# Transposing the feed-forward activations with VectorE blocks and DRAM transfers instead of TensorE

## The chip, the core and the metric

The kernel runs on one core of a Trainium2 chip. Its engines work side by side, each through its own queue of instructions in order: TensorE (PE; PEld is its weight load), VectorE (DVE), ScalarE (ACT), GpSimd (POOL) and SyncE (SP). Transfers are issued from SP's and GpSimd's queues and carried out by the core's 16 DMA engines. An instruction that needs another engine's result, or a transfer's, waits for a semaphore at the head of its queue, and all that stands behind it waits too. The metric is the device time of one execution in microseconds (us).

## The reference

One layer of a diffusion transformer: 256 latent tokens and 256 context tokens of width 2048. Modulated norms, one input projection, two kinds of attention, an output projection, and at the end a gated feed-forward block, which the change concerns:

```python
def swiglu_sublayer(x, shift, scale, gate, norm_g, w_ff_gate, w_ff_up, w_ff_down):
    h = modulate(rms_norm(x, norm_g), shift, scale)
    return x + gate * ((jax.nn.silu(h @ w_ff_gate) * (h @ w_ff_up)) @ w_ff_down)
```

Here h is 256 x 2048, w_ff_gate and w_ff_up are 2048 x 5632, w_ff_down is 5632 x 2048, all float32.

## The kernel before

**Matrix products.** Each product is made of three fast ones: a float32 operand is split into a rounded part "hi" and the rest "lo", and hi x hi, hi x lo and lo x hi are added up in PSUM (lines L236, L237 and L238 in `mm3`). A weight tile of 256 rows x 512 columns is loaded by SP into one of seven buffers `wraw`; ScalarE casts it to `whi` (L231) and VectorE subtracts to `wlo` (L232), three buffers each. The activations are kept transposed, split in hi and lo by `split` (ScalarE L241, VectorE L242).

**One projection.** `project` goes through a product of 256 tokens x 512 columns. A *step* is one weight tile: 2 blocks of 128 rows x 2 token halves (tk 0 and 1) x 3 matmuls = 12 matmuls. With 2048 rows that are 8 steps. At the end `evac` takes the two PSUM tiles. After each step `tick` counts down the work that `after(n, fn)` has put off by n steps, and runs what is due.

**The feed-forward stage.** It goes through 11 groups of 512 columns (cg). In each, `project(w_g)` and `project(w_u)` are 8 steps each: `g_evac` writes silu of the gate product to `act[tk]` (ScalarE), `u_evac` multiplies the up product into it (VectorE). `act[tk]` is 128 tokens x 512 columns, and the down product needs it the other way round, with the columns on the partitions. `turn`, two or three steps later, does that: four TensorE transposes of 128x128 into one PSUM tile `ftp` (L990), then `split` from there into the group's tile `fT`, 512 columns x 128 tokens for each tk. The down product w_ff_down reads `fT` after all groups, in 4 groups of 22 steps.

From the third group on, two pieces of another weight matrix (`w_ada`, tile `ada5`) are loaded at each projection, into the same ring of seven buffers, and added up by VectorE (L432).

**Order.** The code's order is the priority; a scheduler puts each engine's instructions in a fixed order from it and from its own estimate of when each is ready. So an instruction can stand ahead of others that the code has earlier. Transfers that GpSimd issues use eight semaphores in turn: the ninth waits for the first to land.

Of the kernel before, what the change touches and what calls it, by code (L numbers as in the profile page):

```python
# [11 lines left out]
F32 = mybir.dt.float32  # L12
# [5 lines left out]
P = 128  # L18
# [14 lines left out]
DFF = 5632  # L33
LAM_INIT = 0.8 - 0.6 * math.exp(-0.3 * 0)
CG = 512
# [10 lines left out]
def hybrid_block(ctx: ExitStack, tc: tile.TileContext, t: dict, out: bass.AP):  # L46
    nc = tc.nc
# [6 lines left out]
    dram = ctx.enter_context(tc.tile_pool(name="dram", bufs=1, space=bass.MemoryType.DRAM))  # L54
    psum = ctx.enter_context(tc.tile_pool(name="psum", bufs=2, space=bass.MemoryType.PSUM))

    def big_tile(name, dt=F32):
        return big.tile([P, 2048], dt, tag="big", name=name)
# [4 lines left out]
    def tp_ps(name="tp"):  # L63
        return psum.tile([P, CG], F32, tag="tp", bufs=2, name=name)
# [4 lines left out]
    def scratch(name, n=CG, dt=F32, tag="scr", bufs=3):  # L69
        return scr.tile([P, n], dt, tag=tag, bufs=bufs, name=name)  # L70
# [5 lines left out]
    ident = tab.tile([P, P], F32, name="ident")  # L76
# [163 lines left out]
    def split(hi, lo, src):  # L240
        nc.scalar.copy(out=hi, in_=src)  # L241
        nc.vector.tensor_tensor(out=lo, in0=src, in1=hi.bitcast(F32), op=ALU.subtract)  # L242
# [178 lines left out]
    def ada_pieces(a, chunk):  # L421

        for kt, hf in [(kt, hf) for kt in range(NKT) for hf in range(2)]:
            wt = wp.tile([P, 1024], F32, tag="wraw", bufs=WRAW, name="wada2")
            nc.sync.dma_start(out=wt, in_=w_ada[kt * P:(kt + 1) * P, chunk * D + hf * 1024: chunk * D + (hf + 1) * 1024])
            dst = a[:, hf * 1024:(hf + 1) * 1024]
            yield None
            with tc.issue_after(last_lo[-1].ins):
                if kt == 0:
                    nc.vector.tensor_scalar(out=dst, in0=wt, scalar1=sc[:, 0, 0:1], scalar2=None, op0=ALU.mult)  # L430
                else:
                    nc.vector.scalar_tensor_tensor(out=dst, in0=wt, scalar=sc[:, 0, kt:kt + 1], in1=dst, op0=ALU.mult, op1=ALU.add)  # L432
# [94 lines left out]
    def take(gen, n):  # L527
        for _ in range(n):
            if next(gen, gen) is gen:
                return  # L530

    def drain(gen):
        for _ in gen:
            pass
# [9 lines left out]
    def after(n, fn):  # L544
        late.append([n, fn])
# [68 lines left out]
    def project(src, hl, nkt, c0, evac, kt0=0, side=None, head=1, tail=1, hook=None):  # L614


        ps = [mm_ps() for _ in range(2)]
        nt = nkt // WK
        order = [(i, tk) for i in range(nt) for tk in range(2)]
        order[:2 * head] = [(i, tk) for tk in range(2) for i in range(head)]  # L620
        order[-2 * tail:] = [(i, tk) for tk in range(2) for i in range(nt - tail, nt)]
        wt = {}
        for n, (i, tk) in enumerate(order):
            if i not in wt:
                wt[i] = load_w(src, i * WK * P, c0, in_big=WHI <= i < head or nt - tail <= i < nt - WHI)
            wh, wl = wt[i]
            for j in range(WK):
                k = i * WK + j
                ah, al = hl.at(kt0 + k, tk * P, P)
                mm3(ps[tk], ah, al, wh[:, j], wl[:, j], k == 0, k == nkt - 1)  # L630
            if i == nt - 1 and (tail > 1 or tk == 1):
                for x in ([tk] if tail > 1 else range(2)):
                    evac(x, ps[x])
            if hook:
                hook(i, tk)
            if n % 2:
                tick()
                if side:
                    side()
                yield None  # L640
# [24 lines left out]
    def q_evac(qT, br):  # L665
        def f(tk, ps):
            o = norm_rope(ps, br, "q", tk)

            def turn():
                tp = tp_ps("qtp")  # L670
                for h in range(4):
                    nc.tensor.transpose(out=tp[:, h * P:(h + 1) * P], in_=o[:, h * P:(h + 1) * P], identity=ident)
                src = tp.rearrange("p (h q) -> p h q", h=4)
                split(qT[:, 0, :, tk * P:(tk + 1) * P], qT[:, 1, :, tk * P:(tk + 1) * P], src)
            after(5 + tk, turn)
        return f
# [79 lines left out]
    def unit(br, u):  # L756
        return (u // 4, u % 4) if br == "a" else (u // 8, u // 2 % 4)
# [59 lines left out]
    for n, (br, u) in enumerate(units):  # L817
        q = (br, unit(br, u)[0])
# [33 lines left out]
    for cg in range(4):  # L852
# [19 lines left out]
        def gated(tk, ps):  # L872
            g = gs[tk]
            nc.vector.tensor_tensor(out=g, in0=ps, in1=g, op=ALU.mult)
            nc.vector.tensor_tensor(out=m[tk], in0=m[tk], in1=g, op=ALU.add)
            after(2 + tk, turn(tk))

        def turn(tk, cg=cg, m=m):
            def f():
                tp = tp_ps("mtp")  # L880
                for j in range(4):
                    nc.tensor.transpose(out=tp[:, j * P:(j + 1) * P], in_=m[tk][:, j * P:(j + 1) * P], identity=ident)
                hi, lo = mT.four(cg, tk * P, P)
                split(hi, lo, tp.rearrange("p (h q) -> p h q", h=4))
            return f
# [84 lines left out]
    w_g, w_u, w_d = t["w_ff_gate"][0], t["w_ff_up"][0], t["w_ff_down"][0]  # L970
    NFT = DFF // P
    fT = Parts("fT", NFT)
    for cg in range(DFF // CG):
        if cg == 2:
            a5 = big_tile("ada5")
            a5_gen = ada_pieces(a5, 5)
        act = [scratch(f"act{tk}") for tk in range(2)]

        def g_evac(tk, ps):
            nc.scalar.activation(out=act[tk], in_=ps, func=AF.Silu)  # L980

        def u_evac(tk, ps):
            nc.vector.tensor_tensor(out=act[tk], in0=ps, in1=act[tk], op=ALU.mult)
            after(2 + tk, turn(tk))

        def turn(tk, cg=cg, act=act):
            def f():
                tp = tp_ps("ftp")
                for j in range(4):
                    nc.tensor.transpose(out=tp[:, j * P:(j + 1) * P], in_=act[tk][:, j * P:(j + 1) * P], identity=ident)  # L990
                hi, lo = fT.four(cg, tk * P, P)
                split(hi, lo, tp.rearrange("p (h q) -> p h q", h=4))
            return f

        drain(project(w_g, hT, NKT, cg * CG, g_evac, **(dict(head=TURN2, hook=head_hook) if cg == 0 else {})))
        if cg > 1:
            take(a5_gen, 2)
        drain(project(w_u, hT, NKT, cg * CG, u_evac))
        if cg > 1:
            take(a5_gen, 2)  # L1000
# [50 lines left out]
```

## Time and profile before

| | |
|---|---|
| runs | 1722.39, 1725.93 and 1726.39 us, median 1725.93 |
| the profiled execution | 1727.13 us; its span from the first to the last instruction 1725.0 us |
| TensorE | busy 1697.9 us (98% of the span), granted clock 0.999 of full speed |
| VectorE, ScalarE | 1134.0 us (66%), 772.9 us (45%) |
| GpSimd | 134.1 us (8%) |
| DMA | 400.82 MB; SP's queue 66.3% of 16 engines' span, GpSimd's queue 4.9% |

Busy time is the sum of an engine's instructions. Matmuls are pipelined, so a row of the profile gives 390 ns for a matmul of 512 columns while the next one starts 0.23 us after it. In the profile a group of instructions is named by line, engine and operation and by out<-in; `mm` is a PSUM tile of a product, `fT` the transposed activations, `fturn` and `fpart` (in the kernel after) the tiles of the new way. Times given as t are counted from the moment at which TensorE ends an up group.

### The profile page before, as it was taken

How to read it: one execution, taken by the hardware profiler on the slowest of the kernel's cores; microseconds unless marked ns; L12 is line 12 of the kernel's file. 1: busy time of each engine (PE TensorE's matmuls, PEld its weight loads, DVE VectorE, ACT ScalarE, POOL GpSimd, SP SyncE). 2: the span in 40 equal slices, each digit the busy share in tenths (PEclk: the TensorE clock that was granted, in tenths of full speed). 3: DMA queues.
4: the chain of work that ended last, by engine and by line, in shares of the span. 5: the costliest groups of instructions: out<-in, count | busy, mean ns of one | idle time of the engine just before them, and what ended most of it. 6: DMA issues, size and time to landing. Idle time of an engine off the chain costs nothing.

```text
span 1725.0 us, 21768 instructions
## 1 busy us (share of the span) xinstructions
PE 1697.9 (98%) x8110; PEld 1370.6 (79%) x8110; DVE 1134.0 (66%) x1444; ACT 772.9 (45%) x1064; POOL 134.1 (8%) x204
## 2 busy tenths in 40 slices
PE   7999999999999999999999999999999999999998
PEld 5676778877887788887888788888888888888887
DVE  4764779788788979786665754565556565444554
ACT  5221223245666565666544444444444444333332
POOL 2100002011131120002111100000000000000000
PEclk9999999999999999999999999999999999999999
DMA  9987694778756667777787756677777777666662
GB/s 275 314 303 266 238 328 163 222 243 267 248 177 216 224 221 263 225 232 243 253 314 227 228 182 194 208 231 234 241 234 241 234 241 229 210 209 200 219 206 87
DMA packets 192873, 400.82 MB, mean 232 GB/s; under 512 B 13600, under 2 KB 25968, under 8 KB 192256
## 3 DMA queue, kind: packets, MB, share of 16 engines
q1 hardware_dynamic: 184816, 372.86, 66.3%
q0 software_dynamic: 7952, 26.58, 4.9%
q8 instruction: 63, 1.03, 0.2%
q14 instruction: 42, 0.34, 0.1%
HBM read 388.87 MB, written 10.52 MB: 232 GB/s over the span
## 4 chain that ended last, share of the span: by engine, by line
PE 85%; DVE 5%; issue 3%; DMA 3%; ACT 1%; POOL 1%; SPq 1%; ACTq 0%; DVEq 0%; POOLq 0%
PE mm L237 26%; PE mm L236 26%; PE mm L238 26%; DMA wraw<-in_w_in_dram 3%; DVE wlo L232 2%; PE ptp L726 1%; PE ada L292 1%; ACT whi L231 1%; PE o L744 1%; PE ftp L990 1%; PE s L706 1%; PE o L237 0%; PE o L238 0%; PE o L236 0%; PE s L236 0%
## 5 line engine op out<-in xcount | busy, mean ns | idle before, releaser
L232 DVE TENSOR_TENSOR wlo<-wraw,whi 128x1024 fp32r<-128x1024 f32 (+1 forms) x506 | 611.3, 1210 | 465.1 <-ACT whi L231 461.6
L231 ACT CAST whi<-wraw 128x1024 fp32r<-128x1024 f32 (+1 forms) x506 | 527.4, 1043 | 790.1 <-PE mm L238 657.6
L237 PE MATMUL mm<-wlo,hT 128*128 128x512 f32 x696 | 271.2, 390 | 2.0 <-DVE wlo L232 2.0
L236 PE MATMUL mm<-whi,hT 128*128 128x512 f32 x696 | 273.1, 392 | 0.0
L238 PE MATMUL mm<-whi,hT 128*128 128x512 f32 x696 | 271.6, 390 | 0.1
L236 PE MATMUL mm<-whi,xT 128*128 128x512 f32 x640 | 255.9, 403 | 1.4 <-DVE vb L415 0.9
L237 PE MATMUL mm<-wlo,xT 128*128 128x512 f32 x640 | 251.2, 392 | 1.0 <-DVE wlo L232 0.9
L238 PE MATMUL mm<-whi,xT 128*128 128x512 f32 x640 | 250.3, 391 | 0.0
L237 PEld LDWEIGHTS mm<-wlo,hT 128*128 128x128 f32 x696 | 130.9, 188 | 28.9 <-DVE wlo L232 2.4
L238 PEld LDWEIGHTS mm<-whi,hT 128*128 128x128 f32 x696 | 130.8, 188 | 28.0 <-DVE hT L242 0.5
L432 DVE SCALAR_TENSOR_TENSOR ada<-wada,sc,ada 128x1024 f32<-128x1024 f32 x120 | 151.9, 1276 | 0.0
L236 PEld LDWEIGHTS mm<-whi,xT 128*128 128x128 f32 x640 | 119.5, 188 | 40.7 <-issue 11.4
L236 PEld LDWEIGHTS mm<-whi,hT 128*128 128x128 f32 x696 | 130.8, 188 | 26.3
L237 PEld LDWEIGHTS mm<-wlo,xT 128*128 128x128 f32 x640 | 120.4, 188 | 26.9 <-DVE wlo L232 3.3
L238 PEld LDWEIGHTS mm<-whi,xT 128*128 128x128 f32 x640 | 120.1, 188 | 25.8 <-DVE xT L382 0.4
L236 PE MATMUL mm<-whi,fT 128*128 128x512 f32 x352 | 137.2, 390 | 0.0
L238 PE MATMUL mm<-whi,fT 128*128 128x512 f32 x352 | 137.0, 389 | 0.0
L237 PE MATMUL mm<-wlo,fT 128*128 128x512 f32 x352 | 136.9, 389 | 0.0
L236 PEld LDWEIGHTS mm<-whi,fT 128*128 128x128 f32 x352 | 66.1, 188 | 14.5 <-issue 0.8
L238 PEld LDWEIGHTS mm<-whi,fT 128*128 128x128 f32 x352 | 66.1, 188 | 13.9
L237 PEld LDWEIGHTS mm<-wlo,fT 128*128 128x128 f32 x352 | 66.1, 188 | 13.4
L236 PE MATMUL mm<-whi,cT 128*128 128x512 f32 x192 | 75.0, 393 | 1.4 <-ACT cT L381 1.4
(246 smaller groups left out, 2092.0 us busy)
## 6 DMA issues: line engine op xcount, KB each, us to landing
wada<-in_w_ada_dram SPq DMA_DIRECT2D x192, 512.0 KB, 4.8
wraw<-in_w_in_dram SPq DMA_DIRECT2D x154, 512.0 KB, 4.8
wraw<-in_w_ff_gate_dram SPq DMA_DIRECT2D x88, 512.0 KB, 4.3
wraw<-in_w_ff_up_dram SPq DMA_DIRECT2D x88, 512.0 KB, 3.7
wraw<-in_w_ff_down_dram SPq DMA_DIRECT2D x88, 512.0 KB, 4.2
wraw<-in_w_br_a_dram SPq DMA_DIRECT2D x32, 512.0 KB, 5.1
wraw<-in_w_out_dram SPq DMA_DIRECT2D x32, 512.0 KB, 5.8
wraw<-in_w_br_b_dram SPq DMA_DIRECT2D x16, 512.0 KB, 5.9
```

The costliest lines, as they stand in the source:

```text
L231: last_hi.append(nc.scalar.copy(out=hi[:, 0:nk], in_=raw[:, 0:nk]))
L232: last_lo.append(nc.vector.tensor_tensor(out=lo[:, 0:nk], in0=raw[:, 0:nk], in1=hi[:, 0:nk].bitcast(F32), op=ALU.subtract))
L236: nc.tensor.matmul(ps, lhsT=ah, rhs=wh, start=first, stop=False)
L237: nc.tensor.matmul(ps, lhsT=ah, rhs=wl, start=False, stop=False)
L238: return nc.tensor.matmul(ps, lhsT=al, rhs=wh, start=False, stop=last)
L292: last_pe[0] = nc.tensor.matmul(aps[32 * g:32 * g + 32, 0:ncol], lhsT=cst[:, k, :], rhs=rhs, start=(k < 4), stop=(k >= NKT - 4))
L432: nc.vector.scalar_tensor_tensor(out=dst, in0=wt, scalar=sc[:, 0, kt:kt + 1], in1=dst, op0=ALU.mult, op1=ALU.add)
L706: nc.tensor.matmul(sps[i], lhsT=qT[rows, x, hh, tk * P:(tk + 1) * P], rhs=kT["b", grp][y][rows, hh, :], start=(n == 0), stop=(n == 2))
L726: nc.tensor.transpose(out=tp[:, kt * P:(kt + 1) * P], in_=p[:, kt * P:(kt + 1) * P], identity=ident)
L744: nc.tensor.matmul(op[:, 0:BV], lhsT=pT[:, kt, :], rhs=vb[:, kt, hh * BV:(hh + 1) * BV], start=(kt == 0), stop=(kt == 3))
L990: nc.tensor.transpose(out=tp[:, j * P:(j + 1) * P], in_=act[tk][:, j * P:(j + 1) * P], identity=ident)
```

## The change

`turn` is taken out. Instead `u_evac` calls `turned` at once for each tk:

```diff
 def u_evac(tk, ps):
     nc.vector.tensor_tensor(out=act[tk], in0=ps, in1=act[tk], op=ALU.mult)
-    after(2 + tk, turn(tk))
-
-def turn(tk, cg=cg, act=act):
-    def f():
-        tp = tp_ps("ftp")
-        for j in range(4):
-            nc.tensor.transpose(out=tp[:, j * P:(j + 1) * P], in_=act[tk][:, j * P:(j + 1) * P], identity=ident)
-        hi, lo = fT.four(cg, tk * P, P)
-        split(hi, lo, tp.rearrange("p (h q) -> p h q", h=4))
-    return f
+    turned(act[tk], *fT.four(cg, tk * P, P), cg, tk)
...
+turn_d = dram.tile([2 * (DFF // CG), P, CG], F32, name="turn_d")
+
+def turned(src, dst_hi, dst_lo, cg, tk):
+    part = scratch("fpart", tag="nr", bufs=2)
+    nc.vector.transpose(out=part, in_=src)
+    whole = scratch("fturn", tag="sq", bufs=2)
+    held = turn_d[2 * cg + tk]
+    nc.gpsimd.dma_start(out=held, in_=part)
+    blocks = held.rearrange("(a i) (k b j) -> b i k a j", a=4, k=4, b=4)
+    for b in range(4):
+        nc.gpsimd.dma_start(out=whole[32 * b:32 * b + 32].rearrange("p (k a j) -> p k a j", k=4, a=4), in_=blocks[b])
+    after(10 + 2 * tk, lambda: split(dst_hi, dst_lo, whole.rearrange("p (k q) -> p k q", k=4)))
```

VectorE's instruction turns each 32x32 block of the tile in its place. What is left is to move whole blocks to their places. The tile is written to DRAM (128 rows of 2 KB) and read back by four transfers, one for each 32 partitions of the result; a row of a block is 32 floats, so each read is made of 512 pieces of 128 bytes. The split comes 10 steps (tk 0) or 12 (tk 1) after the up product in the code, not 2 and 3. The buffers `nr` and `sq` are not used by anything else at that time, and there are two of each, one per tk.

What the orders show. TensorE, at the end of the first step of a gate group (here the sixth; `mm` are PSUM tiles, `whi` and `wlo` weights, `hT` the input). Before:

```order
L238 MATMUL mm_10539<-whi_10542,hT0_8873 128x512
L236 MATMUL mm_10539<-whi_10542,hT0_8873 128x512
L237 MATMUL mm_10539<-wlo_10543,hT0_8873 128x512
L238 MATMUL mm_10539<-whi_10542,hT0_8873 128x512
L990 MATMUL ftp_10558<-ident_75,act0_10211 128x128 x4
L236 MATMUL mm_10538<-whi_10568,hT0_8873 128x512
L237 MATMUL mm_10538<-wlo_10569,hT0_8873 128x512
```

After:

```order
L238 MATMUL mm_10581<-whi_10584,hT0_8873 128x512
L236 MATMUL mm_10581<-whi_10584,hT0_8873 128x512
L237 MATMUL mm_10581<-wlo_10585,hT0_8873 128x512
L238 MATMUL mm_10581<-whi_10584,hT0_8873 128x512
L236 MATMUL mm_10580<-whi_10602,hT0_8873 128x512
L237 MATMUL mm_10580<-wlo_10603,hT0_8873 128x512
```

The four transposes are gone, and nothing has come in their place; the same holds one step later and in each of the 11 groups.

ScalarE in that gate group and the start of the up group, whose steps are counted on as 0 to 15. Before, from whi of step 2 (whi_10593):

```order
L231 CAST whi_10593<-wraw_10591 128x1024
L231 CAST whi_10611<-wraw_10609 128x1024
L241 CAST fT4_10563<-ftp_10558 128x4x128
L231 CAST whi_10629<-wraw_10627 128x1024
L241 CAST fT4_10563<-ftp_10584 128x4x128
L231 CAST whi_10647<-wraw_10645 128x1024
```

After, from whi of step 5 (whi_10674):

```order
L231 CAST whi_10674<-wraw_10672 128x1024
L231 CAST whi_10692<-wraw_10690 128x1024
L241 CAST fT4_10554<-fturn_10557 128x4x128
L231 CAST whi_10710<-wraw_10708 128x1024
L231 CAST whi_10738<-wraw_10736 128x1024
L241 CAST fT4_10554<-fturn_10566 128x4x128
L231 CAST whi_10758<-wraw_10756 128x1024
L994 ACTIVATE act0_10578<-mm_10580 128x512
```

The cast of tile 0 has moved from behind whi of step 3 to a place between whi of steps 6 and 7, that of tile 1 to a place between steps 8 and 9. Both now wait for four transfers each.

VectorE from the products at the end of the up group on. Before:

```order
L983 TENSOR_TENSOR act0_10211<-mm_10382,act0_10211 128x512
L983 TENSOR_TENSOR act1_10212<-mm_10383,act1_10212 128x512
L232 TENSOR_TENSOR wlo_10594<-wraw_10591,whi_10593 128x1024
L232 TENSOR_TENSOR wlo_10612<-wraw_10609,whi_10611 128x1024
L242 TENSOR_TENSOR fT4_10563<-ftp_10558,fT4_10563 128x4x128
L232 TENSOR_TENSOR wlo_10630<-wraw_10627,whi_10629 128x1024
L242 TENSOR_TENSOR fT4_10563<-ftp_10584,fT4_10563 128x4x128
```

After, the same place (wlo_10621 is step 2's) and, following the mark, the stretch with the splits:

```order
L997 TENSOR_TENSOR act0_10247<-mm_10403,act0_10247 128x512
L997 TENSOR_TENSOR act1_10248<-mm_10404,act1_10248 128x512
L978 STREAM_TRANSPOSE fpart_10555<-act0_10247 128x512
L978 STREAM_TRANSPOSE fpart_10564<-act1_10248 128x512
L232 TENSOR_TENSOR wlo_10621<-wraw_10618,whi_10620 128x1024
...
L242 TENSOR_TENSOR fT4_10554<-fturn_10557,fT4_10554 128x4x128
L232 TENSOR_TENSOR wlo_10711<-wraw_10708,whi_10710 128x1024
L432 SCALAR_TENSOR_TENSOR ada5_9585<-wada2_10576,sc_103,ada5_9585 128x1024
L432 SCALAR_TENSOR_TENSOR ada5_9585<-wada2_10729,sc_103,ada5_9585 128x1024
L232 TENSOR_TENSOR wlo_10739<-wraw_10736,whi_10738 128x1024
L242 TENSOR_TENSOR fT4_10554<-fturn_10566,fT4_10554 128x4x128
L232 TENSOR_TENSOR wlo_10759<-wraw_10756,whi_10758 128x1024
```

Both block transposes stand ahead of wlo of step 2. The split of tile 0 now stands ahead of wlo of step 7, the two additions to ada5 and wlo of step 8.

GpSimd, which had nothing in the gate and up groups but one row load, now has ten transfers in each group, in this order in the last two groups:

```order
L981 DMA turn_d_8924<-fpart_12210 128x512
L981 DMA turn_d_8924<-fpart_12219 128x512
L984 DMA fturn_12212<-turn_d_8924 32x16x32 x4
L984 DMA fturn_12221<-turn_d_8924 32x16x32 x4
L440 DMA adac_sb_12553<-in_b_ada_dram 32x512 x4
L981 DMA turn_d_8924<-fpart_12536 128x512
L981 DMA turn_d_8924<-fpart_12545 128x512
L454 DMA row_d_118<-adac_sb_12553 4x512
L984 DMA fturn_12538<-turn_d_8924 32x16x32 x4
L984 DMA fturn_12547<-turn_d_8924 32x16x32 x4
L458 DMA a5_12565<-row_d_118 128x2048
```

Both writes are issued before the first read, which waits for the first write to land; in the last group the row transfers of `a5` stand among them. The order of SP's loads is as before.

## The prediction

> **What bounds the kernel now.** I read the page's chain first, then the stretch that the change touches by windows, then its waits, then single instructions. The chain that ended last, by engine:
>
> ```profile
> PE 85%; DVE 5%; issue 3%; DMA 3%; ACT 1%; POOL 1%; SPq 1%; ACTq 0%; DVEq 0%; POOLq 0%
> ```
>
> The feed-forward part runs from about 1010 us to the end. One column group of its gate and up projections takes 44 us; the windows give one such stretch, with one near the start where the DMA engines were full, and the waits of 1000 to 1490 us (who waited for whom: total us, times, longest):
>
> ```profile
> core 0: us, PE busy (x) PEld busy (x) DVE busy (x) ACT busy (x) POOL busy (x), PEclk, DMA share, GB/s
> 15.00:20.00 5.00, 3.13 (x24) 2.58 (x23) 3.79 (x14) 2.91 (x8) 0.66 (x2) 1.00 1.06 387
> ...
> 1188.00:1232.00 44.00, 44.00 (x200) 36.44 (x199) 26.60 (x24) 18.47 (x21) 0.00 (x0) 1.00 0.73 236
> ...
> ACT whi L231 <- PE mm L238: 271.4, 165, 4.3
> DVE wlo L232 <- ACT whi L231: 212.4, 159, 4.2
> ```
>
> TensorE is busy 44.00 of 44.00 us at full clock; ScalarE waits for it, VectorE for ScalarE, and nothing else waits long. So here a microsecond taken from TensorE is a microsecond of the kernel, as long as weights keep coming.
>
> **What is removed.** The rows of the tile ftp (min/median/max ns), and TensorE's timeline about one set of four:
>
> ```profile
> L990 PEld LDWEIGHTS ftp<-ident,act x88: 138/138/139, 1036.1 to 1485.5; 128*128 128x128 f32 x88
> L990 PE MATMUL ftp<-ident,act x88: 271/272/273, 1036.3 to 1485.6; 128*128 128x128 f32 x88
> L241 ACT CAST fT<-ftp x22: 579/579/580, 1037.5 to 1486.4; 128x512 fp32r<-128x512 f32 x22
> L242 DVE TENSOR_TENSOR fT<-ftp,fT x22: 681/682/684, 1038.8 to 1487.7; 128x512 fp32r<-128x512 f32 x22
> ...
> 1080.33 0.39 PE L237 MATMUL mm<-wlo,hT 128*128 128x512 f32 x1
> 1080.56 0.39 PE L238 MATMUL mm<-whi,hT 128*128 128x512 f32 x1
> 1080.79 0.60 PE L990 MATMUL ftp<-ident,act 128*128 128x128 f32 x4
> 1081.14 0.47 PE L236 MATMUL mm<-whi,hT 128*128 128x512 f32 x1
> 1081.45 0.39 PE L237 MATMUL mm<-wlo,hT 128*128 128x512 f32 x1
> ```
>
> Matmuls start 0.227 us apart (1080.33 to 1080.56). From L238 at 1080.56 to L237 at 1081.45 are 0.89 us where two such steps would be 0.45: the four transposes cost 0.44 us, not 4 x 0.27, since they are pipelined. ScalarE's clockwork, which follows TensorE's steps, gives the same in a second way:
>
> ```profile
> 1167.17 1.06 ACT L231 CAST whi<-wraw 128x1024 fp32r<-128x1024 f32 x1 [1.67 <-PE mm L238]
> 1169.89 1.05 ACT L231 CAST whi<-wraw 128x1024 fp32r<-128x1024 f32 x1 [1.67 <-PE mm L238]
> 1170.85 0.58 ACT L241 CAST fT<-ftp 128x512 fp32r<-128x512 f32 x1
> 1173.08 1.05 ACT L231 CAST whi<-wraw 128x1024 fp32r<-128x1024 f32 x1 [1.65 <-PE mm L238]
> ```
>
> A step of 12 matmuls is 2.72 us (1167.17 to 1169.89), one with transposes 3.19: 0.47 more. I take 0.46; 22 tiles x 0.46 = 10.1 us. That is all there is to gain.
>
> **What is added on VectorE.** Two block transposes a group. The trace has none; VectorE's row of the same size, and its longest common one, bound it:
>
> ```profile
> L983 DVE TENSOR_TENSOR act<-mm,act x22: 678/681/683, 1033.3 to 1478.5; 128x512 f32<-128x512 f32 x22
> ...
> L432 DVE SCALAR_TENSOR_TENSOR ada<-wada,sc,ada 128x1024 f32<-128x1024 f32 x120 | 151.9, 1276 | 0.0
> ...
> 1161.24 2.47 DVE L432 SCALAR_TENSOR_TENSOR ada<-wada,sc,ada 128x1024 f32<-128x1024 f32 x2
> 1163.63 1.22 DVE L232 TENSOR_TENSOR wlo<-wraw,whi 128x1024 fp32r<-128x1024 f32 x1
> 1165.54 1.23 DVE L232 TENSOR_TENSOR wlo<-wraw,whi 128x1024 fp32r<-128x1024 f32 x1 [0.69 <-ACT whi L231]
> 1166.68 1.28 DVE L983 TENSOR_TENSOR act<-mm,act 128x512 f32<-128x512 f32 x2
> 1168.26 1.23 DVE L232 TENSOR_TENSOR wlo<-wraw,whi 128x1024 fp32r<-128x1024 f32 x1 [0.30 <-ACT whi L231]
> ```
>
> Take 0.68 each (same elements), between nothing and 1.28. Let t = 0 be the end of an up group on TensorE, 1167.1 here. The two products end at 0.9, the transposes at 1.5 and 2.2, and the wlo of step 2, which began at 1.2, ends at 3.5 instead of 2.4. TensorE needs it at 2 x 2.72 = 5.44. Hidden by 1.9 us, at 1.28 still by 0.7; past 1.6 us each it is not. The two splits stay, from SBUF instead of PSUM: ScalarE casts 1024 elements from SBUF in 1.05, so 512 in about 0.6; same cost.
>
> **What is added on GpSimd and the DMA queues.** Ten transfers a group: two writes of 128 rows of 2 KB, eight reads of 512 pieces of 128 bytes (32 partitions x 16). Nothing of this size of piece is in the trace. Landing times of its GpSimd transfers (us from issue), what GpSimd spends on an issue (mean ns), and two stretches of the queues (q1 is SP's, q0 GpSimd's; packets, MB, share of 16 engines), one with 512-byte packets alone (4 to 6 us), one with GpSimd's small loads (29 to 45 us):
>
> ```profile
> gin<-gate_d POOLq DMA_DIRECT2D x16, 256.0 KB, 4.8
> x_d<-xn POOLq DMA_DIRECT2D x8, 256.0 KB, 5.1
> xr<-x_d POOLq DMA_DIRECT2D x8, 256.0 KB, 6.4
> out_dram<-y POOLq DMA_DIRECT2D x6, 256.0 KB, 3.9
> wraw<-in_w_ff_gate_dram SPq DMA_DIRECT2D x88, 512.0 KB, 4.3
> ...
> L767 POOL DMA_DIRECT2D gate_d<-gate x16 | 9.2, 572 | 59.8 <-ACT gate L766 58.5 <-ACT o L754 1.1 <-issue 0.2
> L187 POOL DMA_DIRECT2D cs<-in_rope_a_dram x1 | 0.7, 741 | 0.0
> ...
> DMA packets 1156, 0.58 MB, mean 292 GB/s; under 512 B 16, under 2 KB 1156, under 8 KB 1156
> q1 hardware_dynamic: 1156, 0.58, 101.7%
> ...
> DMA packets 4316, 3.80 MB, mean 238 GB/s; under 512 B 288, under 2 KB 3846, under 8 KB 4313
> q1 hardware_dynamic: 3945, 3.18, 65.3%
> q0 software_dynamic: 368, 0.59, 37.7%
> ```
>
> - Issue: 0.57 us for 128 pieces, 0.74 for 256. Going on by 0.17 per 128, 512 pieces take 1.1 us; the low end is 0.57.
> - Engine time of a piece: 1156 packets of 512 bytes kept 16 engines busy for 2 us, 28 ns each. At 387 GB/s a 2 KB packet is 85 ns. A line through both gives 14 ns for 128 bytes: the low end. The high end is GpSimd's own queue at the start: 37.7% of 16 engines for 16 us, 96.5 us, over 12 loads of 1664 pieces in all (nine of 128 rows would be 1152, the two rope tables have 256 each): 58 ns. Those loads are mostly one DRAM row copied to 128 partitions; the new reads have distinct addresses, as the 512-byte packets have, so I take 28. A tile's 2048 pieces are 128 per engine: 3.6 us (1.8 to 7.4).
>
> The clock of a group: write 0 goes out at 1.6 and lands 3.9 to 5.1 later; with 4.5 that is 6.1. GpSimd issues the eight reads from there, the fourth at 9.4, the eighth at 13.8. With the 4.8 to 6.4 of its reads they land at 14.2 to 15.8 (tile 0) and 18.6 to 20.2 (tile 1).
>
> **Who waits for that.** The orders show what the diff does not: the cast of tile 0 stands on ScalarE ahead of whi of step 7, not after step 8, and tile 1's ahead of step 9. ScalarE reaches the first at about 12 (whi of step 6 begins when step 3 ends, 10.9). If the data is there at L, the cast takes 0.6, whi 1.05, wlo 1.22; then VectorE has two ada additions (2.5) and the wlo of step 8, ending at L + 6.6, which TensorE wants at 8 x 2.72 + 0.2 = 22.0. So L may be 15.4 (16.4 in the groups without ada). For tile 1: cast, whi and wlo of step 9 by 24.7, so 21.8.
>
> By engine time instead of landing rows: from 7.2 (the first issue over) to 12 the reads get the 27% that weights leave, 1.3 of 3.6 us; then ScalarE stands still, no weight buffer is freed, no load starts, and the rest takes 2.3: 14.3. Tile 1 shares with two weight loads (2 x 1.35): 14.3 + 3.6 + 2.7 = 20.6. Both are in time, by about 1 us, and ScalarE's own wait is paid from its lead of two steps.
>
> The engines' total: 256 pieces x 28 ns + 16 rows x 85 ns = 8.5 us in 44, 19% on top of 73%: 92%, where 106% was seen at full. Weights have seven buffers; 16 weight and 4 ada loads share them in 16 steps, so a load goes out 5.6 steps (15.2 us) less the two conversions (2.4) before its use, 12.8 us, and lands in 4.3: 8.5 us of lead. Hidden. In the last group the a5 row load stands behind the reads; it is first used 22 steps later.
>
> Sum: 1727.13 (the profiled execution, span 1725.0 and 2.1 around it) - 10.1 = 1717.0. The median of the runs, 1725.93, is 1.2 below the profiled one; the same saving from there is 1715.8.
>
> **Rivals.**
> 1. *The reads land late and ScalarE's queue passes it on* (slower). With 58 ns a piece, tile 0 has 7.4 us of engine time: 1.3 by 12, the rest by 18.1, 2.7 past 15.4. Tile 1 ends 18.1 + 7.4 + 2.7 = 28.2 against 21.8 + 2.7: 3.7 more. 11 groups x 6.4 = 70, less 10: 1787. At 40 ns the two are 0.4 and 1.4 late: 20 - 10, 1737. The break-even is 0.92 us a group, about 37 ns a piece. For it: GpSimd's queue is the one in question. Against: its loads there read the same row again and again.
> 2. *The losses eat the gain* (no change): 0.5 to 1.4 us late a group, pieces of 35 to 39 ns. About 1725.
> [...]
> 4. GpSimd needs over 1.6 us for an issue: the eighth read then goes out after 17.3 and lands past 21.8. At 2.2 us, 26.3 at best, 4.5 late: 50 - 10, 1767.
>
> **How the numbers follow.** The forecast has 0.47, rival 2 0.14, rival 1 0.27, rival 3 0.06, rival 4 0.06. A difference of 0.3% (5 us) is about what a measurement of this kernel can tell from no change: faster 0.47, same 0.14, slower 0.39. The forecast's own range is 1711 to 1721 (the runs lie 4 us apart). Up to 1775 only the upper part of rival 1 and little of 3 and 4 is left out.
>
> **What would show it.** Right: TensorE still 44 of 44, no L990, a group of 43.5 us instead of 44.4, ScalarE's waits for fturn short. Wrong: gaps of TensorE behind wlo, whose chain leads to ScalarE's cast of fT and a DMA fturn; landing of fturn over 6 us; a q0 packet of 32 pieces over 1.2 us; an issue over 1.6 us; waits of whi for wraw.

## The result, and the profile after

| | before | after |
|---|---|---|
| median of 6 runs, us | 1725.43 | 1713.83 |
| lowest to highest, us | 1722.39 to 1726.83 | 1712.59 to 1715.47 |
| profiled execution (span), us | 1727.13 (1725.0) | 1712.62 (1710.8) |

The ratio is 0.9937, with a 95% interval of 0.9927 to 0.9947. The kernel became faster by 0.6%, 11.6 us between the medians; 10.1 were forecast.

In the changed kernel L978 is the stream transpose, L981 the write to DRAM, L984 the four reads of a tile, L994 the silu; the lines before the change keep their numbers. First one group by windows in the columns used before (busy us with instructions of TensorE, its weight load, VectorE, ScalarE and GpSimd, then clock, DMA share, GB/s), then who waited for whom from 1000 to 1490 us:

```profile
1185.00:1229.00 44.00, 44.00 (x196) 36.44 (x195) 27.71 (x26) 19.49 (x21) 7.00 (x10) 1.00 0.89 270
...
ACT whi L231 <- PE mm L238: 241.2, 155, 4.3
POOL fturn L984 <- DMA turn_d<-fpart: 30.6, 11, 3.5
ACT fT L241 <- DMA fturn<-turn_d: 25.4, 17, 2.9
```

TensorE is still busy 44.00 of 44.00 us at full clock. New are 7 us of issuing on GpSimd and a DMA share of 0.89 where it was 0.73. ScalarE now waits 25.4 us for the reads, and no row has TensorE waiting behind that. The rows of the new tiles and of the silu (min/median/max ns, first and last start):

```profile
L978 DVE STREAM_TRANSPOSE fpart<-act x22: 667/687/702, 1030.6 to 1466.4; 128x512 f32<-128x512 f32 x22
L981 POOL DMA_DIRECT2D turn_d<-fpart x22: 547/570/594, 1031.6 to 1467.4; - x22
...
L984 POOL DMA_DIRECT2D fturn<-turn_d x88: 703/961/1336, 1034.2 to 1475.3; - x88
L241 ACT CAST fT<-fturn x22: 616/621/624, 1042.0 to 1484.5; 128x512 fp32r<-128x512 f32 x22
DMA to landing us min/median/max: 3.4/6.0/9.5
...
L994 ACT ACTIVATE act<-mm x22: 585/600/602, 1007.7 to 1443.3; 128x512 f32<-128x512 f32 x22
```

The silus are a clock for the groups: the first stands in group 0, the last in group 10, so ten groups lie between them. Here that is 1443.3 - 1007.7 = 435.6 us. The same row before reads:

```profile
L980 ACT ACTIVATE act<-mm x22: 593/600/600, 1011.7 to 1456.6; 128x512 f32<-128x512 f32 x22
```

That is 444.9: 9.3 more, 0.93 a group, 10.2 over eleven. From the second group on, the silus of a tile lie 44.45 us apart before and 43.52 (once 43.55) after; the prediction had 44.4 and 43.5. The two profiled spans differ by 14.2, of which 4.0 lie ahead of the first silu (1011.7 against 1007.7), where nothing was changed.

Then the clock of one group, on GpSimd, ScalarE and VectorE. The end of its up group on TensorE, t = 0 in the prediction's count, is at 1160.3:

```profile
1162.12 0.58 POOL L981 DMA_DIRECT2D turn_d<-fpart  x1 [33.68 <-DVE fpart L978]
...
1166.66 5.85 POOL L984 DMA_DIRECT2D fturn<-turn_d  x8 [3.19 <-DMA turn_d<-fpart]
...
1174.87 0.62 ACT L241 CAST fT<-fturn 128x512 fp32r<-128x512 f32 x1 [2.52 <-DMA fturn<-turn_d]
...
1179.01 0.62 ACT L241 CAST fT<-fturn 128x512 fp32r<-128x512 f32 x1 [1.22 <-DMA fturn<-turn_d]
...
1177.62 2.48 DVE L432 SCALAR_TENSOR_TENSOR ada<-wada,sc,ada 128x1024 f32<-128x1024 f32 x2
1180.01 1.22 DVE L232 TENSOR_TENSOR wlo<-wraw,whi 128x1024 fp32r<-128x1024 f32 x1
```

The cast of tile 0 starts at t = 14.6, that of tile 1 at 18.7, each as soon as its reads have landed. What follows is the stretch that the prediction had put at 6.6 us: the two ada additions and the wlo of step 8, which ends at 1181.2, t = 20.9. TensorE wants it at 22.0. So this group has about 1 us to spare. The others are much alike: in the ten groups that a gate group follows, the cast of tile 0 starts at t = 12.3 to 14.9 and that of tile 1 at 17.4 to 19.1, so the least that is left to the deadline of 15.4 is 0.5 us.

### The profile page after: what moved, and what is told of

Its sections match the earlier page's. It is cut to its first block, busy times and chain, and to the rows that moved or that the text cites. A ratio compares the mean times of both kernels' runs of the same rounds, so it can differ in the third digit from the quotient of the medians.

```text
span 1710.8 us, 21865 instructions
## 1 busy us (share of the span) xinstructions
PE 1686.9 (99%) x8022; PEld 1362.2 (80%) x8022; DVE 1145.9 (67%) x1466; ACT 774.5 (45%) x1064; POOL 211.4 (12%) x314
## 3 DMA queue, kind: packets, MB, share of 16 engines
q8 instruction: 63, 1.03, 0.2%
## 4 chain that ended last, share of the span: by engine, by line
PE 83%; DVE 7%; DMA 4%; issue 4%; ACT 1%; POOL 1%; SPq 1%; ACTq 0%; DVEq 0%; POOLq 0%
PE mm L236 25%; PE mm L237 25%; PE mm L238 25%; DMA wraw<-in_w_in_dram 3%; DVE wlo L232 2%; PE ada L292 1%; PE ptp L726 1%; ACT whi L231 1%; PE o L744 1%; PE s L706 1%; DVE nr L484 0%; PE o L237 0%; DVE ss L469 0%; PE o L238 0%; PE o L236 0%
## 5 line engine op out<-in xcount | busy, mean ns | idle before, releaser
L237 PEld LDWEIGHTS mm<-wlo,fT 128*128 128x128 f32 x352 | 66.1, 188 | 13.8
L238 PE MATMUL mm<-whi,oT 128*128 128x512 f32 x192 | 74.9, 391 | 1.3 <-DVE oT L242 1.3
```

Of the source, the lines that this page charges most:

```text
L237: nc.tensor.matmul(ps, lhsT=ah, rhs=wl, start=False, stop=False)
L238: return nc.tensor.matmul(ps, lhsT=al, rhs=wh, start=False, stop=last)
```

## The experiments

Each states its edit against the changed kernel. Times are medians with the lowest and highest run; ratios are to the kernel before, run on the same chip (1723.7 to 1724.0 there).

### Without the transfers

The split reads the VectorE blocks where they stand. The ten transfers of a group, and with them the moving of the blocks to their places, are left out.

```diff
-        whole = scratch("fturn", tag="sq", bufs=2)
-        ...
-        after(10 + 2 * tk, lambda: split(dst_hi, dst_lo, whole.rearrange("p (k q) -> p k q", k=4)))
+        after(10 + 2 * tk, lambda: split(dst_hi, dst_lo, part.rearrange("p (k q) -> p k q", k=4)))
```

> Leaves out all ten transfers of a group: the split reads the tile that VectorE has turned block by block, so the blocks are not moved to their places. Theory (TensorE's 22 sets of transposes were the whole cost, the transfers are hidden): the same time as the changed kernel, 1713.8 us, ratio to before 0.993 to 0.995; TensorE 44 of 44 us in a group. Rival (the transfers, or ScalarE's 25 us of waits for them, still cost something that TensorE's rows don't show): 1711 us or less, ratio below 0.992.

Measured: 1712.53 us (1711.23 to 1713.66), ratio 0.9936 [0.9923, 0.9948]. The silus of ten groups lie 435.6 us apart, as with the transfers:

```profile
L988 ACT ACTIVATE act<-mm x22: 592/598/598, 1009.2 to 1444.8; 128x512 f32<-128x512 f32 x22
```

So the ten transfers of a group cost nothing that can be measured.

### TensorE's transposes put back beside the new way

```diff
+        def on_pe():
+            tp = tp_ps("ftp")
+            for j in range(4):
+                nc.tensor.transpose(out=tp[:, j * P:(j + 1) * P], in_=src[:, j * P:(j + 1) * P], identity=ident)
+        after(2 + tk, on_pe)
```

Nothing reads their result.

> The changed kernel, with TensorE's four transposes per tile done as before as well, into a PSUM tile that nobody reads. Theory: the transfers cost nothing, so all of the gain goes: 1725.4 us as before, ratio 0.999 to 1.001, a group of 44.4 us. Rival (transposes on TensorE are partly free, the gain came from elsewhere, such as the earlier release of PSUM or a shorter wait): it stays below 1722, ratio under 0.998. Rival (transfers cost something): over 1728.

Measured: 1724.56 us (1722.75 to 1726.13), ratio 1.0004 [0.9995, 1.0013]: the whole gain is gone. Ten groups take 444.9 us again, the figure of before to a tenth:

```profile
L1000 ACT ACTIVATE act<-mm x22: 590/600/602, 1007.7 to 1452.6; 128x512 f32<-128x512 f32 x22
...
ACT fT L241 <- DMA fturn<-turn_d: 5.7, 6, 1.6
```

The two runs together show that the gain is the 88 transposes on TensorE, 0.46 us for four, and nothing else. The wait of ScalarE falls from 25.4 to 5.7 us here: TensorE's steps with transposes take longer, so ScalarE comes to the casts later (to tile 0 no sooner than t = 12.9, to tile 1 at 18.3, where the changed kernel has 12.3 and 17.4).

### The splits earlier

The cast of tile 0 is forced ahead of whi of step 5 (in the changed kernel: step 7), that of tile 1 ahead of step 7 (step 9).

```diff
     def load_w(...)
-        last_hi.append(nc.scalar.copy(out=hi[:, 0:nk], in_=raw[:, 0:nk]))
+        if ahead:
+            with tc.issue_after(ahead.pop().ins):
+                last_hi.append(nc.scalar.copy(out=hi[:, 0:nk], in_=raw[:, 0:nk]))
+        else:
+            ...
-        after(10 + 2 * tk, lambda: split(...))
+        def put():
+            view = whole.rearrange("p (k q) -> p k q", k=4)
+            ahead.append(nc.scalar.copy(out=dst_hi, in_=view))
+            nc.vector.tensor_tensor(out=dst_lo, in0=view, in1=dst_hi.bitcast(F32), op=ALU.subtract)
+        after(6 + 2 * tk, put)
```

> The changed kernel with the two splits forced ahead in the queues: tile 0's cast ahead of whi of step 5 (it stands ahead of step 7), tile 1's ahead of step 7 (of step 9). Theory (a cast that waits at the head of ScalarE's queue is paid from TensorE's lead of two steps, and beyond that by TensorE): the data lands at t = 13.5 to 14.5, wlo of step 5 follows 2.9 us later, TensorE wants it at 13.8, so 2.6 to 3.6 us a group, 11 groups: 29 to 40 us over the changed kernel, 1743 to 1754 us, ratio 1.010 to 1.017. Rival (ScalarE's waits cost nothing, there is slack elsewhere): 1714 us.

Measured: 1752.69 us (1749.0 to 1755.45), ratio 1.0168 [1.0151, 1.0184]. That is 38.9 us over the changed kernel, 3.5 for each of the eleven groups, at the upper end of what was expected. The waits from 1000 to 1490 us (all lines stand some lower in this kernel: L240 to L242 are the matmuls, L992 the cast), the silus' row, ScalarE's row in one group with t = 0 at 1172.6, TensorE's rows there, and windows:

```profile
ACT fT L992 <- DMA fturn<-turn_d: 70.4, 11, 8.0
PE mm L240 <- ACT whi L233: 14.4, 10, 2.5
PE mm L241 <- DVE wlo L236: 4.6, 9, 0.5
...
L1003 ACT ACTIVATE act<-mm x22: 590/600/600, 1010.8 to 1484.4; 128x512 f32<-128x512 f32 x22
...
1186.52 0.62 ACT L992 CAST fT<-fturn 128x512 fp32r<-128x512 f32 x1 [7.32 <-DMA fturn<-turn_d]
...
1185.88 0.39 PE L242 MATMUL mm<-whi,hT 128*128 128x512 f32 x1
1188.14 0.73 PE L240 MATMUL mm<-whi,hT 128*128 128x512 f32 x2 [1.87 <-ACT whi L233]
1189.40 0.50 PE L241 MATMUL mm<-wlo,hT 128*128 128x512 f32 x1 [0.53 <-DVE wlo L236]
1191.62 0.63 PE L242 MATMUL mm<-whi,hT 128*128 128x512 f32 x1
1192.05 0.63 PE L240 MATMUL mm<-whi,hT 128*128 128x512 f32 x1
...
1190.00:1192.00 2.00, 2.00 (x6) 1.57 (x5) 2.00 (x3) 0.50 (x1) 0.00 (x0) 0.50 0.70 168
```

The data lands at about the same moment as in the changed kernel (t = 13.9 here, 14.6 there), but ScalarE now stands 7.3 us for it with step 5 behind it, its lead of two steps is used up, and TensorE stands 1.87 and 0.53 us. The matmul that needs the wlo of step 5 starts at 1189.40, t = 16.8, 3.0 us later than TensorE wants it. This is rival 1's mechanism, with the reads no slower than they were: the deadline makes it. A second loss follows the first. After those two pauses the granted clock is 0.50 and matmuls start 0.43 us apart (1191.62 to 1192.05) instead of 0.227, from about 1190.0 to 1193.3; eight matmuls at 0.20 more are 1.6 us. The rows of TensorE show such a slow stretch in seven of the eleven groups. The two losses together account for the time: in the first ten groups the cast starts at t = 13.6 on average, 2.9 and the deadline of 13.8 make that 2.7 us a group, 27 in all, and seven slow stretches are 11; by the silus ten groups take 473.6 us, 38.0 more than in the changed kernel. The waits alone would be 30 us in eleven groups, the low end of what was expected; the slow clock, which was not expected, brought the sum to the upper end.

### The splits later

The splits are held behind the whi and wlo that the code has just issued, so the casts stand behind whi of steps 8 and 10.

```diff
-        after(10 + 2 * tk, lambda: split(...))
+        def put():
+            view = whole.rearrange("p (k q) -> p k q", k=4)
+            with tc.issue_after(last_hi[-1].ins):
+                nc.scalar.copy(out=dst_hi, in_=view)
+            with tc.issue_after(last_lo[-1].ins):
+                nc.vector.tensor_tensor(out=dst_lo, in0=view, in1=dst_hi.bitcast(F32), op=ALU.subtract)
+        after(10 + 2 * tk, put)
```

> The changed kernel with the two splits forced back in the queues: tile 0's cast behind whi of step 8, tile 1's behind whi of step 10. Theory (the waits of ScalarE were paid from the lead): ScalarE's waits for fturn go from 25 us to under 3, and the time stays at 1713.8 us, ratio 0.993 to 0.995. Rival (the waits cost part of the gain): 1711 us or less, ratio below 0.992.

Measured: 1713.99 us (1710.96 to 1714.58), ratio 0.9941 [0.9929, 0.9954]. The waits of ScalarE have no row for the tile any more; what was there is back in the wait for TensorE:

```profile
ACT whi L231 <- PE mm L238: 268.4, 169, 4.3
```

25.4 us of waits taken away change nothing: in the changed kernel they were paid from ScalarE's lead, entirely.

### The reads twice, and four times

Spare reads of the same blocks go out ahead of the real ones, into a tile that nothing reads: four a tile in one kernel, twelve in the other.

```diff
+        spare = scratch("fspare", tag="pTb", bufs=2)
+        for b in range(4):
+            nc.gpsimd.dma_start(out=spare[32 * b:32 * b + 32].rearrange("p (k a j) -> p k a j", k=4, a=4), in_=blocks[b])
```

> The changed kernel with each tile read twice: four spare reads into a tile that nobody uses stand ahead of the four real ones, so 16 reads a group; the order puts the two casts later (tile 0's between whi of steps 8 and 9, tile 1's some steps behind). Theory (the DMA engines have room: a group's share rose from 0.73 to about 0.88, of which 0.03 are the writes, so a second set of reads brings it to about 1.00 where 1.06 to 1.15 were seen at full; the lead of the weight loads covers the burst): 1714 us, ratio 0.993 to 0.996. Rival (weights starve behind the small pieces): TensorE waits for wlo and whi for wraw, 1722 us or more.

> As the one before, with each tile read four times (32 reads a group, 8192 pieces of 128 bytes beyond the writes over and above the 4096 of two reads). Theory A (a set of reads costs the engines the 0.12 by which the share rose): 0.73 + 0.03 + 4 x 0.12 = 1.24 where 1.06 is full, so a group with ada takes 51 us instead of 43.5 and the kernel about 1780 to 1790 us, with whi waiting for wraw. Theory B (a piece costs only the 10 ns that the rows of GpSimd's queue give, 62 us of engine time a group less 22 for the writes, over 4096 pieces): four sets are 10 us per engine and group, everything stays hidden, 1714 to 1718 us.

Measured: with twice the reads 1714.13 us (1712.38 to 1715.86), ratio 0.9947 [0.9932, 0.9961]; with four times 1768.81 us (1766.36 to 1774.24), ratio 1.0265 [1.0247, 1.0283]. The queues in one group (packets, MB, share of 16 engines) of the changed kernel, then with twice the reads, with a wait and a landing time of that kernel:

```profile
q1 hardware_dynamic: 5100, 10.82, 79.7%
q0 software_dynamic: 416, 1.05, 8.8%
```

```profile
1188.00:1232.00 44.00, 44.00 (x196) 36.45 (x195) 27.70 (x26) 19.51 (x21) 12.73 (x18) 1.00 0.96 269
...
q1 hardware_dynamic: 4796, 10.23, 80.3%
q0 software_dynamic: 672, 1.57, 15.5%
...
ACT whi L231 <- DMA wraw<-in_w_ff_up_dram: 10.0, 6, 2.7
wraw<-in_w_ff_up_dram SPq DMA_DIRECT2D x88, 512.0 KB, 8.3
```

Beside them, SP's queue in the version without the transfers:

```profile
q1 hardware_dynamic: 5097, 10.82, 78.3%
```

4096 more pieces of 128 bytes add 6.7% of 16 engines for 44 us (704 us in all) in their own queue: 47 us, 11.5 ns a piece. The weights' packets beside them also take longer, 110 ns each in the changed kernel (79.7% of 704 us over 5100) and 118 with twice the reads; put down to the pieces, that is 4796 x 8 = 38 us or 9 ns more, some 20 in all. That is the price of the second set, in a stretch that is 96% full. The first set cost the weights far less: without any reads their packets take 108 ns, 2 less, which is 2 to 3 ns a piece. The weights of the up product now land in 8.3 us after their issue, where the changed kernel has 5.2, and ScalarE begins to wait for them (10.0 us). Their lead is nearly used up, and TensorE is still busy throughout. The casts also stand later in this kernel, tile 0 behind step 8, so it tells nothing about the deadline of the split. With four times the reads the weights do starve:

```profile
1188.00:1232.00 44.00, 41.14 (x169) 33.26 (x168) 23.02 (x22) 15.55 (x17) 21.55 (x31) 0.92 1.04 273
...
ACT whi L231 <- DMA wraw<-in_w_ff_gate_dram: 51.7, 23, 6.1
```

The DMA engines are full (1.04) and TensorE loses 3 us of 44 and some of its clock (0.92). But most of the loss lies elsewhere. The silus are no clock here, since their places on ScalarE moved; the down product's matmuls are. Their rows in the changed kernel and in this one, and from this one the splits and one stretch:

```profile
L238 PE MATMUL mm<-whi,fT x352: 388/389/395, 1466.5 to 1705.2; 128*128 128x512 f32 x176
...
L238 PE MATMUL mm<-whi,fT x352: 387/389/632, 1482.8 to 1759.0; 128*128 128x512 f32 x176
L241 ACT CAST fT<-fturn x22: 610/618/622, 1060.9 to 1599.3; 128x512 fp32r<-128x512 f32 x22
...
1530.00:1605.00 75.00, 54.43 (x168) 35.58 (x167) 20.41 (x20) 16.82 (x18) 28.64 (x42) 0.86 0.62 165
```

The down product starts 16 us later than in the changed kernel and takes 37 us longer. From 1530 to 1605 us TensorE is busy 54.4 of 75 us, at a clock of 0.86, while the DMA engines are at 0.62 and nothing waits for `wraw`: there TensorE waits for whi and wlo, and ScalarE for TensorE, in turn. The last splits stand in the same stretch (1599.3, where the changed kernel has 1484.5). Why TensorE and ScalarE lose their lead on each other there stays open. So starving weights explain at most the 16 us ahead of the down product. The time lies between what the two theories gave, but the larger part of the loss follows from neither.

### The same way for the gated merge

Three of four groups of the merge ahead of the output projection, six tiles, go by the same path, with the split seven (tk 0) or nine (tk 1) steps later; `turned` moves ahead of the merge and is given the number of steps.

```diff
-            after(2 + tk, turn(tk))
+            if cg < 3:
+                turned(m[tk], *mT.four(cg, tk * P, P), DFF // CG + cg, tk, wait=7)
+            else:
+                after(2 + tk, turn(tk))
```

> The changed kernel, with the same way of transposing also for the first three of the four column groups of the gated merge (six tiles; the last group keeps TensorE, since the output projection follows at once). Theory (TensorE is as full there, 0.46 us a tile): 6 x 0.46 = 2.8 us less, 1711 us, ratio 0.991 to 0.993. Rival (GpSimd's queue, which loads the gates there, stands 3 to 4 us at the head for the write, and the gates or the splits come late): 1714 us or more.

Measured: 1716.53 us (1711.86 to 1718.33), ratio 0.9952 [0.9939, 0.9965]. The theory gave too much; the time is the rival's. From 866 to 900 us in the changed kernel, then in this one, and a wait of this one from 790 to 990:

```profile
866.00:900.00 34.00, 34.00 (x159) 28.16 (x159) 22.44 (x26) 16.68 (x20) 5.36 (x10) 1.00 0.91 333
```

```profile
866.00:900.00 34.00, 31.97 (x140) 25.30 (x139) 21.88 (x27) 17.09 (x21) 13.48 (x22) 1.00 1.03 304
...
ACT mT L241 <- DMA fturn<-turn_d: 15.6, 6, 5.0
```

There the DMA engines were 91% busy without the new transfers. With them they are full (1.03), ScalarE stands up to 5 us for the reads, and TensorE is idle for 2 us of the 34. That takes back most of the 2.8 us of transposes saved (6 x 0.46). What makes the splits late isn't separated: full DMA engines, GpSimd's own queue (it stands up to 3.4 us for a write here), or the smaller number of steps. Whether the kernel is slower than with the feed-forward part alone isn't told: the intervals overlap.

### The transfers from SP's queue, and the silu's place

```diff
-        nc.gpsimd.dma_start(out=held, in_=part)
+        nc.sync.dma_start(out=held, in_=part)
```

and the four reads likewise.

> The changed kernel with the ten transfers of a group issued by SP, whose queue also loads the weights, instead of GpSimd. Theory (SP stands about 3 to 4 us for the write to land and some 4 us for the issues, within the 8.5 us by which loads run ahead): 1714 to 1717 us, ratio 0.993 to 0.996. Rival (the weight loads behind the waiting read come late): gaps of TensorE of 2 us and more in each group, 1735 us or more.

Measured: 1743.87 us (1742.7 to 1745.27), ratio 1.0116 [1.0103, 1.0129]; the time is the rival's, but the mechanism is neither's: nothing waits long for `wraw`. Two of the waits, and one stretch of ScalarE:

```profile
ACT act L994 <- PE mm L238: 49.8, 17, 5.2
PE mm L236 <- ACT whi L231: 11.6, 8, 1.6
...
1181.53 0.62 ACT L241 CAST fT<-fturn 128x512 fp32r<-128x512 f32 x1
1187.38 0.60 ACT L994 ACTIVATE act<-mm 128x512 f32<-128x512 f32 x1 [5.23 <-PE mm L238]
1189.23 2.93 ACT L231 CAST whi<-wraw 128x1024 fp32r<-128x1024 f32 x3
```

The casts of the tile wait for nothing. What ScalarE waits for, up to 5.2 us, is the products of the next group's gate, for its silu: in this order the silu stands right behind the cast of tile 1 and ahead of the next whi, so that ScalarE stops until TensorE ends the gate group, and then does three whi in a row, too late for TensorE. The next kernel is the same with the silu held behind the whi that the code has just issued:

```diff
-            nc.scalar.activation(out=act[tk], in_=ps, func=AF.Silu)
+            def silu(tk=tk, ps=ps, act=act):
+                with tc.issue_after(last_hi[-1].ins):
+                    nc.scalar.activation(out=act[tk], in_=ps, func=AF.Silu)
+            after(3, silu)
```

> The version whose ten transfers SP issues, with one thing put back: the silu of the gate product stands behind whi of step 9 on ScalarE, as in the changed kernel (in the SP version the order had it ahead of whi of step 8, where it waits for the end of the gate product). Theory (the SP version lost its time through that place of the silu, not through SP's queue): 1714 to 1717 us, ratio 0.993 to 0.996, ScalarE's waits for the gate product back from 50 us to about 10. Rival (SP's queue, which holds weight loads back while it waits for the write): still 1735 us or more, with waits for wraw.

Measured: 1714.04 us (1711.37 to 1715.17), ratio 0.9946 [0.9929, 0.9963], with TensorE busy throughout and ScalarE's waits for the gate product back at 9.8 us:

```profile
1188.00:1232.00 44.00, 44.00 (x196) 36.44 (x195) 28.18 (x27) 19.00 (x20) 0.00 (x0) 1.00 0.85 265
```

So the 30 us between the two runs were the silu's place, not the queue. Which queue carries the transfers makes no difference to the time here (ratio 0.9946 from SP's, 0.9937 from GpSimd's).

### Four steps instead of ten in the code

```diff
-        after(10 + 2 * tk, lambda: split(...))
+        after(4 + 2 * tk, lambda: split(...))
```

> The changed kernel with the splits put off by 4 and 6 steps in the code, not 10 and 12. The casts stand at the same places of ScalarE's order, ahead of whi of steps 7 and 9. Theory (the scheduler's own estimate of the landing sets the place, and the place sets the time): 1714 us, ratio 0.993 to 0.996. Rival (the number of steps in the code matters): a stall as where the casts were forced ahead, 1740 us or more.

Measured: 1714.14 us (1712.47 to 1715.99), ratio 0.9945 [0.993, 0.996]. ScalarE's instructions stand in the same order as with ten. So the number in the code is not what places the split here; that the scheduler's estimate of when the data is there does it is likely, but not shown by itself.

This run also shows where the deadline lies. In one of its groups (t = 0 at 1204.7) the reads land later than in any other, and the cast of tile 0 starts at t = 16.0:

```profile
1220.70 0.62 ACT L241 CAST fT<-fturn 128x512 fp32r<-128x512 f32 x1 [3.92 <-DMA fturn<-turn_d]
...
1225.84 1.22 DVE L232 TENSOR_TENSOR wlo<-wraw,whi 128x1024 fp32r<-128x1024 f32 x1
...
1226.40 0.39 PE L236 MATMUL mm<-whi,hT 128*128 128x512 f32 x1
1227.11 0.50 PE L237 MATMUL mm<-wlo,hT 128*128 128x512 f32 x1 [0.32 <-DVE wlo L232]
```

That is 0.6 past the prediction's 15.4, and TensorE's matmul that needs the wlo of step 8 starts 0.71 us after the one ahead of it instead of 0.23: 0.5 late.

## Why the prediction was right

- **What is removed** was sized right. 0.46 us for four transposes gave 10.1; the silus give 10.2, and putting the transposes back brings exactly that back (444.9 for ten groups). The pipelined step, not the 271 ns of each row, is the price: 88 x 0.271 would be 23.8. The 1.4 us by which the medians differ beyond this is less than the runs' own spread.
- **VectorE's blocks** took 687 ns where 0.68 was taken. They begin at t = 0.8 and are hidden as the count had it.
- **The landing** came out at 14.6 and 18.7, in the group shown, for 14.2 to 15.8 and 18.6 to 20.6, partly because errors cancelled; in half of the groups tile 0 is earlier than that range. The write landed in 3.7 us at the median (4.5 was taken), the reads were issued 0.73 us apart (5.85 for eight; the rows of single issues overlap, 0.96 at the median; 1.1 was taken), and they landed in 6.0 (4.8 to 6.4). So half of the reads showed one of the prediction's signs of being wrong, a landing of over 6 us: by itself it was no sign, since the earlier issue made up for it.
- **The price of a piece** was the term that was sized wrong: 11.5 ns in its own queue, and with what the weights' packets lose beside it some 13 for the first set of reads and 20 for a second, where 28 was taken. Rival 1's break-even of 37 ns was therefore far away and its 0.27 too high. What misled was the nearest row by size, the 512-byte packets of SP's queue. The row that gave the high end, 58 ns, was also misread a little: 11 loads stand there, not 12. The total of the DMA engines, 0.89 for 0.92, shows little of the error, since the weights' queue was busier than before, and not through the reads (73.0% before, 78.3% without the transfers, 79.7% with them).
- **The deadline**, 15.4 for tile 0, was right in kind and size: nothing is lost while the cast starts by 14.9, half a microsecond is lost when it starts at 16.0 (four steps in the code), and with the casts two steps earlier, which brings the deadline to 10.9 (13.8 less 2.9), TensorE stands in every group.
- **ScalarE's wait** of 25.4 us is paid from its lead, as reckoned; the kernel with the splits later shows it. It is longer than the prediction's signs said (short).
- **Rival 3**, that the weights starve, needs four times the reads, and even there explains at most 16 of 54 us. In the changed kernel the weights' loads of the up product slowed down a little (in one group 5.5 us to landing at the median, 4.2 without the transfers), and nothing waited for them. How the DMA engines divide their time between the two queues, which the rival's 0.06 depends on, isn't shown by any run.
- **Rivals 2 and 4** did not occur. An issue at 0.73 us stands far from rival 4's 1.6.

No version that was run beats the changed kernel: four others (splits later, twice the reads, SP's queue with the silu held back, four steps) lie between 1713.99 and 1714.14, and the merge adds nothing.

## What to carry to other kernels

Where TensorE is busy all the time, price what is taken off it by the step from start to start (here 0.46 us for four transposes), not by the duration in its row (0.27 each), and then ask of the replacement only one thing: when its result is first needed, and by whom it is queued ahead of. The waits of ScalarE were free here within its lead (25.4 us in the changed kernel) and stopped TensorE beyond it (1.87 and 0.53 us in one group, with the casts two steps earlier), so count the deadline through the queue (cast, whi, wlo, whatever else VectorE has), and look in the order of instructions for what was moved along with the edit. A transfer that was free in a stretch with 73% busy DMA engines gained nothing in one with 91%.

## What the runs showed of the hardware

- **After short pauses the clock fell to half.** With the splits earlier, after pauses of 1.87 and 0.53 us that end 1.3 us apart, TensorE's granted clock was 0.50 for 3.3 us. It did not happen each time. In that run and in the one with SP's queue, 14 of the 15 groups in which the first pause was 1.07 us or longer had a slow stretch after it (one with 1.60 hadn't), and none of the four in which it was 0.74 or shorter. It added some 1.6 us to a delay of 3.0. Whether the pause alone decides it isn't shown.
- **Small pieces are cheap here.** 128 bytes with distinct addresses cost 11.5 ns of an engine, or some 20 with the slowing of the packets beside them when the engines were 96% full; a 512-byte packet alone in SP's queue cost 28. Whether the addresses matter wasn't tested.
- **The reads landed sooner from SP's queue.** The same reads landed in 2.8 us at the median from SP's queue (with the silu held back) and in 6.0 from GpSimd's, with TensorE never idle and the weight loads beside them in both. It moved the time by nothing.
